# Latent weights summed by contiguous adds on two engines, and value products in fewer, larger batches

## The chip, the cores and the metric

The kernel runs on one core of one Trainium2 chip. The metric is device time in microseconds (us). Engines are named as in the profile: PE (TensorE's products), PEld (its weight loads), DVE (VectorE), ACT (ScalarE), POOL (GpSimd) and SP (SyncE, which issues all DMAs here). A name such as SPq means that engine's queue.

## The reference

One layer of a hybrid trunk over 1024 latent tokens (a grid of 16 rows by 64 columns) and 256 context tokens, width 1024, in float32: a gated feed-forward half step, two token mixers side by side, a merge, and a second half step. The two mixers matter here. Neighbourhood attention has 8 heads of width 64; each query attends to a window of 8 x 16 tokens and to all context tokens. Latent attention has 8 heads; each of the 1024 queries attends to all 1280 keys:

```python
def _attend(q, k, v):
    s = jnp.einsum('bqhd,bkhd->bhqk', q * q.shape[-1] ** -0.5, k).astype(jnp.float32)
    p = jax.nn.softmax(s, axis=-1).astype(v.dtype)
    return jnp.einsum('bhqk,bkhd->bqhd', p, v)
```

The kernel computes the softmax's denominator beside the value product, and divides at the end.

## The kernel before, in words

The program is written in Tile: a step-by-step plan fixes the order on some engines, and the framework orders the rest by priority and readiness and places all waits. PE's products are pinned to the order in which the program names them, and so are the DMAs on SP. The latent loop's operations on DVE, ACT and Pool that are called as `nc.vector`, `nc.scalar` and `nc.gpsimd` are not pinned.

**The latent stage** (about 1473 to 1790 us of the profile) works through 16 items, two per head, each with 512 queries. Keys lie on the partitions: an item has ten key blocks of 128, and so ten steps, kb = 0 to 9. A step does this:

- `scores(kb)`: three products into a PSUM bank ("bs", three banks), then on ACT the exponential into one of ten 128x512 parts (L1979). Five parts share one buffer X of 128x2560; there are four such buffers.
- one product for the maxima of a later item into a bank "bm" (three banks, shared with transposes), and DVE's reduction of it (L1938). An item has ten of them. The last one that item i+1 needs comes in step 4 of item i.
- `follow(i, kb)`: whatever is due at this step. In the kernel before: at step 0 the previous item's `total` (a strided sum of its parts 5 to 9 on DVE, L1993, and the add of Pool's sum of parts 0 to 4, L1994); at step 2 the previous item's second half of the value products, `weigh(1)`, and the products of the total with ones, which lay the denominator out for the division; at step 4 its `out` (reciprocal L2010 and product L2011 on DVE, then copies and subtractions on ACT and Pool); at steps 1 to 4 Pool's adds of the item's own parts (L1989); at step 5 the next item's `shift`, three short DVE operations over its maxima (L1957 to L1959); at step 6 its `row`, and then the first half of the own value products, `weigh(0)`.
- `row()` turns the shift into a row by a PE transpose (L160), copies it on DVE (L1966) and sends it by four small DMAs into row 96 of the query tile. The next item's first score product reads that row.

A value product multiplies a part (two halves of 256 queries) with 64 value columns, and the two halves go to the two halves of the PSUM bank's partitions ("bv", two banks). Each is seen as two entries in the profile, so that five parts show as x20.

**The neighbourhood stage** (about 1345 to 1470 us) works through 32 items, one per head and block of 16 query columns. A pair of items shares an X buffer and a bank "bv". An item transposes its weights in three parts (`local`, `context`, `edge`), copies them to SBUF tiles and remembers the value products as jobs. When the item's three parts are done and two more parts have followed, its `weigh` does the jobs, 20 entries of PE. Behind the odd item of a pair follows the pair's `out`. Scores of later items stand between the parts.

Durations named here for the stages are read off the timeline.

Of the kernel before, what the change touches and what calls it, by code (L numbers as in the profile page):

```python
# [12 lines left out]
ALU = mybir.AluOpType  # L13
AX = mybir.AxisListType

P = 128
# [22 lines left out]
def f32(ap):  # L39
    return ap.bitcast(F32)  # L40
# [3 lines left out]
def hybrid_block(ctx: ExitStack, tc: tile.TileContext, a: dict, out: bass.AP):  # L44
    nc = tc.nc
# [10 lines left out]
    def nm(s):  # L56
        count[0] += 1
        return f"{s}_{count[0]}"
# [17 lines left out]
    def T2(dt=F32, n=512):  # L76
        return pools["t"].tile([P, n], dt, tag="t", name=nm("t"))
# [13 lines left out]
    def PB(tag):  # L91
        return ps.tile([P, 512], F32, tag=tag, name=nm("b" + tag), bufs=PBUFS[tag])
# [22 lines left out]
    class Engine:  # L115


        def __init__(self, e):
            self.e = e
# [36 lines left out]
    def mmul(o, s, m, start, stop):  # L156
        return pin(nc.tensor.matmul(o, s, m, start=start, stop=stop, skip_group_check=open_group[0]))  # L157

    def turn_(o, x, i):
        return pin(nc.tensor.transpose(o, x, i))  # L160
# [96 lines left out]
    ones = strip[:, 1:2]  # L257
# [1017 lines left out]
    def emit_cq(i, ci, x, bank):  # L1275

        t, q = x, T2()
        if bank:
            t = T2()
            act.copy(t, x)  # L1280
        act.activation(q, t, AF.Square)
        if ci in sq:
            vec.tensor_tensor(sq[ci], sq[ci], q, op=ALU.add)
        else:
            sq[ci] = q
        store(cqx[i, :, ci * 512:(ci + 1) * 512], t)
# [22 lines left out]
    for p in range(3):  # L1309
        punits.append(Unit(h2, [cq_src(2 * p), cq_src(2 * p + 1)],  # L1310
                           lambda i, ci, x, bank, p=p: emit_cq(2 * p + i, ci, x, bank)))
# [451 lines left out]
    def weigh(pv, c, vts, pts, start, stop):  # L1763


        open_group[0] = True
        for e in range(2):
            n = pts[e].shape[-1]
            mmul(pv[64 * e:64 * e + 64, c:c + n], vts[e], pts[e], start, stop)
        open_group[0] = False  # L1770
# [3 lines left out]

    class NaPair:
        def __init__(self):
            self.x, self.pv = None, []

        def scores(self, n):
            if n < EARLY:  # L1780
# [26 lines left out]
    na_pairs = [NaPair() for _ in range(NH * 2)]  # L1807

    class NaItem:
# [38 lines left out]
        def weigh(self, last=True):  # L1848
            pv = na_pairs[self.n // 2].bank(self.n)
            for i, (vts, t) in enumerate(self.jobs):  # L1850
                weigh(pv, (self.n % 2) * P, vts, (t[:, 0:P], t[:, P:2 * P]), not self.begun, last and i == len(self.jobs) - 1)
                self.begun = True
            self.jobs = []

        def values(self):
            hd, j, h, pr = self.head, self.j, self.head.h, self.pr
            vt = lambda g: hd.v[:, j * 256 + g * 64:j * 256 + g * 64 + 64]
            vc = lambda g: f32(hd.kvc[:, 256 + g * 64:320 + g * 64])

            def turned(blocks, t, eng, tag="m"):  # L1860
                n = P * len(blocks)
                pb = PB(tag)
                for x, (s, kb) in enumerate(blocks):
                    turn_(pb[:, x * P:(x + 1) * P], pr[s][:, kb * P:(kb + 1) * P], ident)
                (nc.scalar.copy if eng else nc.vector.tensor_copy)(t[:, :n], pb[:, :n])

            def local():
                t = T2()
                turned(((0, 1), (1, 0), (0, 2), (1, 1)), t, 1, "m" if self.n else "v")
                self.jobs += [((vt(1 + e),) * 2, t[:, e * 256:(e + 1) * 256]) for e in range(2)]  # L1870

            def context():
                t = T2()
                turned(((0, 3), (1, 3), (0, 4), (1, 4)), t, 0, "s" if self.n == 1 else "m")
                self.jobs += [((vc(e),) * 2, t[:, e * 256:(e + 1) * 256]) for e in range(2)]

            def edge():
                t = T2()
                turned(((0, 0), (1, 2)), t, 1)
                self.jobs.append(((vt(0), vt(3)), t))  # L1880
                return [self.weigh] + ([lambda: na_pairs[self.n // 2].out(self.n, h, j)] if self.n % 2 else [])

            return [local, context, edge]

# [40 lines left out]
    class MlaItem:  # L1925
# [58 lines left out]
        def add(self, kb):  # L1984


            if kb == 1:
                self.acc = T2()
            nc.gpsimd.tensor_tensor(self.acc, self.part(0) if kb == 1 else self.acc, self.part(kb), op=ALU.add)  # L1989

        def total(self):
            self.l = T2()
            nc.vector.tensor_reduce(self.l, self.pt[1].rearrange("p (k q) -> p q k", k=5), axis=AX.X, op=ALU.add)  # L1993
            nc.vector.tensor_tensor(self.l, self.l, self.acc, op=ALU.add)  # L1994

        def weigh(self, half):
            if half == 0:
                self.pv = PB("v")
            for kb in range(5 * half, 5 * half + 5):
                v = self.hd.v[:, kb * 64:(kb + 1) * 64]  # L2000
                x = self.part(kb)
                weigh(self.pv, 0, (v, v), (x[:, 0:256], x[:, 256:512]), kb == 0, kb == 9)
            if half:
                v = ones.to_broadcast([P, 64])
                weigh(self.pv, 256, (v, v), (self.l[:, 0:256], self.l[:, 256:512]), True, True)

        def out(self):
            t, h, pv = T2(), self.hd.h, self.pv
# [142 lines left out]
    def follow(i, kb):  # L2151


        prev = mla[i - 1] if i else None
        item = mla[i] if i < len(mla) else None
        after = mla[i + 1] if i + 1 < len(mla) else None
        if kb == 0 and prev:
            prev.total()
        if kb == 0 and i % 2 == 0 and i // 2 + 1 < NH:
            mla_heads[i // 2 + 1].second()  # L2160
        if kb == 2 and prev:
            prev.weigh(1)
        if kb == 4 and prev:
            prev.out()
        if item and 1 <= kb < 6:
            item.add(kb) if kb < 5 else None
        if after and kb == 5:
            after.shift()
        if kb == 5 and i % 2 and i // 2 + 2 < NH:
            mla_heads[i // 2 + 2].first()  # L2170
        if after and kb == 6:
            after.row()
        if item and kb == 6:
            item.weigh(0)

    for i, item in enumerate(mla):
        for kb in range(10):
            item.scores(kb)
            next(tops, None)
            if i == 0:  # L2180
                finish_one()
                if pending and kb % 2 == 0:
                    ending += pending.pop(0)
            follow(i, kb)
            if i >= 14 and kb == 0:
                fm.load(i - 14)
            if i >= 14 and kb == 5:
                fm.split()
    for kb in range(5):
        follow(len(mla), kb)  # L2190
        for _ in range(3 if kb < 2 else 2):
            if fm.left:
                fm.step()
# [264 lines left out]
```

## Time and profile before

| what | value |
|---|---|
| runs | 2585.33, 2587.09, 2595.04 us; median 2587.09 |
| profiled execution | 2595.56 us, its span 2593.8 us |
| granted TensorE clock | 0.991 mean |
| busy | PE 97%, DVE 73%, ACT 43%, POOL 10% |
| chain that ended last | PE 87%, DVE 9%, ACT 2% |

The busy shares are means over stages with different limits, so they tell little of the latent stage alone. In a row of the timeline stand start, duration, engine, line, operation, the tile written and those read, shape and count, and in brackets how long the engine stood idle before it and who released it. Line L157 is the helper of all products and L123 that of pinned operations; the tiles tell them apart.

### The profile page before, as it was taken

Reading aid. Unit: us, or ns where it says so; the run is one execution under the profiler, and the core shown is the slowest. Engines: PE = TensorE matmul, PEld = TensorE weight load, DVE = VectorE, ACT = ScalarE, POOL = GpSimd, SP = SyncE. Lnnn points to the kernel's source line nnn. Section 1 sums busy time; section 2 is a strip of 40 time slices with the busy share of each in tenths; the row PEclk is TensorE's granted clock in tenths of the full one; section 3 lists DMA queues with packets and bytes.
Section 4 is the critical chain, followed back from the end, with each engine's and each line's share of the span. In section 5 each row is a group of like instructions: output and inputs, shape, how many; then the busy total and the mean of one; then the engine's idle time right before and its main releaser. Section 6 shows DMA issues by size and latency. Waiting matters only on the chain.

```text
span 2593.8 us, 36835 instructions
## 1 busy us (share of the span) xinstructions
PE 2521.7 (97%) x13176; PEld 2073.4 (80%) x13176; DVE 1893.2 (73%) x3146; ACT 1121.3 (43%) x2007; POOL 255.3 (10%) x368
## 2 busy tenths in 40 slices
PE   8999999999999999999999988889999999999998
PEld 6888888888998888888888755556888888888887
DVE  4789986797775578863557677676886888767777
ACT  5633223446654753433537533332167322333444
POOL 1000000001100000001003344332011000000003
PEclk9999999999999999999999999999999999999999
DMA  8555543943664666765867422214846444336824
GB/s 303 157 175 192 190 151 126 340 134 130 235 257 155 238 217 208 257 212 125 269 230 246 131 53 55 53 29 173 314 159 227 150 159 158 114 107 222 282 71 162
DMA packets 247671, 464.73 MB, mean 179 GB/s; under 512 B 61056, under 2 KB 77632, under 8 KB 247488
## 3 DMA queue, kind: packets, MB, share of 16 engines
q1 hardware_dynamic: 247488, 462.38, 53.3%
q8 instruction: 104, 1.70, 0.3%
q14 instruction: 79, 0.65, 0.1%
HBM read 341.59 MB, written 120.65 MB: 178 GB/s over the span
## 4 chain that ended last, share of the span: by engine, by line
PE 87%; DVE 9%; ACT 2%; issue 1%; DMA 1%; SPq 0%; POOL 0%; POOLq 0%; DVEq 0%; ACTq 0%
PE bs L157 37%; PE bm L157 27%; PE bv L157 20%; DVE t L1993 3%; DVE st L1938 2%; PE bm L160 2%; DVE t L2010 1%; PE bs L160 1%; ACT t L123 1%; DVE xv L123 1%; DVE xu L123 1%; ACT xu L123 0%; DVE t L1994 0%; DVE t L123 0%; PE bv L160 0%
## 5 line engine op out<-in xcount | busy, mean ns | idle before, releaser
L123 ACT CAST xu<-t 128x512 fp32r<-128x512 f32 (+1 forms) x270 | 160.9, 601 | 494.1 <-DVE t L123 352.4
L157 PE MATMUL bm<-xu,xu 128*128 128x512 f32 (+2 forms) x1572 | 366.5, 386 | 0.0
L157 PE MATMUL bs<-xv,xu 128*128 128x512 f32 x1488 | 357.3, 389 | 0.3 <-DVE t L123 0.3
L157 PE MATMUL bv<-xv,xu 128*128 128x512 f32 x1342 | 335.5, 389 | 0.0
L157 PEld LDWEIGHTS bm<-xu,xu 128*128 128x128 f32 x1572 | 288.1, 188 | 56.6 <-ACT t L123 0.2
L157 PEld LDWEIGHTS bs<-xv,xu 128*128 128x128 f32 x1488 | 279.2, 188 | 59.0 <-issue 1.1
L157 PEld LDWEIGHTS bv<-xv,xu 128*128 128x128 f32 x1342 | 251.8, 188 | 52.2
L157 PE MATMUL bs<-xv,xv 128*128 128x512 f32 x1086 | 265.8, 390 | 0.0
L123 DVE TENSOR_TENSOR xu<-xu,xu 128x512 fp32r<-128x512 f32 (+1 forms) x296 | 201.9, 687 | 74.3 <-ACT xu L123 74.0
L157 PEld LDWEIGHTS bs<-xv,xv 128*128 128x128 f32 x1086 | 203.0, 188 | 41.7
L157 PE MATMUL bs<-xu,xu 128*128 128x512 f32 (+1 forms) x972 | 226.2, 382 | 0.0
L123 POOL TENSOR_SCALAR st<-st 128x1 f32<-128x1 f32 (+1 forms) x66 | 34.7, 526 | 1884.3 <-ACT t L123 1866.0
L123 DVE TENSOR_TENSOR t<-t,t 128x512 f32<-128x512 f32 (+2 forms) x278 | 185.2, 673 | 45.0 <-ACT t L123 35.7
L157 PEld LDWEIGHTS bs<-xu,xu 128*128 128x128 f32 x972 | 177.4, 188 | 35.7 <-issue 1.4
L157 PE MATMUL bs<-w,w 96*128 96x512 f32 (+1 forms) x736 | 197.0, 384 | 1.9 <-DMA w<-kr 1.3
L123 DVE TENSOR_TENSOR xu<-t,xu 128x512 fp32r<-128x512 f32 (+1 forms) x270 | 179.3, 664 | 10.7 <-ACT xu L123 10.6
L1979 ACT ACTIVATE xp<-bs 128x512 f32<-128x512 f32 x160 | 95.5, 597 | 205.1 <-PE bs L157 204.5
L157 PE MATMUL bm<-xv,xv 128*128 128x512 f32 x690 | 182.8, 390 | 0.0
L123 ACT CAST xv<-t 128x512 fp32r<-128x512 f32 x170 | 105.7, 622 | 167.0 <-PE bv L157 69.2
L123 DVE TENSOR_TENSOR xv<-t,xv 128x512 fp32r<-128x512 f32 x170 | 117.0, 688 | 65.4 <-ACT xv L123 65.0
L123 ACT CAST xu<-xu 128x512 fp32r<-128x512 f32 x218 | 132.6, 618 | 67.4 <-DMA xu<-in_wo 54.3
L1938 DVE TENSOR_REDUCE st<-bm 128x1 f32<-128x512 f32 (+1 forms) x160 | 105.7, 679 | 74.3 <-PE bm L157 74.3
(242 smaller groups left out, 3935.9 us busy)
## 6 DMA issues: line engine op xcount, KB each, us to landing
d<-t SPq DMA_DIRECT2D x366, 256.0 KB, 2.6
t<-d SPq DMA_DIRECT2D x274, 256.0 KB, 3.7
xu<-in_f1w SPq DMA_DIRECT2D x59, 512.0 KB, 4.1
xu<-in_f2w SPq DMA_DIRECT2D x58, 512.0 KB, 3.9
t<-in_wada SPq DMA_DIRECT2D x112, 256.0 KB, 5.0
xv<-in_f1w SPq DMA_DIRECT2D x44, 512.0 KB, 6.8
xu<-in_winT SPq DMA_DIRECT2D x38, 512.0 KB, 4.8
xu<-in_f1w SPq DMA_DIRECT2D x50, 256.0 KB, 5.4
```

What stands on the lines that cost most here:

```text
L123: return lambda *x, **y: pin(f(*x, **y))
L157: return pin(nc.tensor.matmul(o, s, m, start=start, stop=stop, skip_group_check=open_group[0]))
L160: return pin(nc.tensor.transpose(o, x, i))
L1938: nc.vector.tensor_reduce(d[:, c:c + pb.shape[-2]], pb, axis=AX.X, op=ALU.max)
L1979: nc.scalar.activation(self.part(kb), pb, AF.Exp)
L1993: nc.vector.tensor_reduce(self.l, self.pt[1].rearrange("p (k q) -> p q k", k=5), axis=AX.X, op=ALU.add)
L2010: nc.vector.reciprocal(rb, pv[:, 256:512])
```

## The change

In the latent stage the denominator's sum is spread: Pool adds parts 0 to 6 as they come (six adds instead of four), DVE adds parts 7, 8 and 9 by contiguous adds and then Pool's sum (three adds in place of the strided sum and one add). Each own part is added one step later. The value products of an item are no longer split in two halves at step 6 of the item and step 2 of the next; all ten parts and the products with ones come in one batch at step 3 of the next item. In the neighbourhood stage both items of a pair do their value products together, when the odd item's turn comes.

```diff
     class NaPair:
         def __init__(self):
-            self.x, self.pv = None, []
+            self.x, self.pv, self.items = None, [], []
+
+        def weigh(self):
+            for x in self.items:
+                x.weigh()
...
-                return [self.weigh] + ([lambda: na_pairs[self.n // 2].out(self.n, h, j)] if self.n % 2 else [])
+                pair = na_pairs[self.n // 2]
+                pair.items.append(self)
+                return [pair.weigh, lambda: pair.out(self.n, h, j)] if self.n % 2 else []
...
         def add(self, kb):
+            p = self.part(kb)
             if kb == 1:
                 self.acc = T2()
-            nc.gpsimd.tensor_tensor(self.acc, self.part(0) if kb == 1 else self.acc, self.part(kb), op=ALU.add)
+                nc.gpsimd.tensor_tensor(self.acc, self.part(0), p, op=ALU.add)
+            elif kb < 7:
+                nc.gpsimd.tensor_tensor(self.acc, self.acc, p, op=ALU.add)
+            elif kb == 8:
+                self.l = T2()
+                nc.vector.tensor_tensor(self.l, self.part(7), p, op=ALU.add)
+            elif kb > 8:
+                nc.vector.tensor_tensor(self.l, self.l, p, op=ALU.add)
 
         def total(self):
-            self.l = T2()
-            nc.vector.tensor_reduce(self.l, self.pt[1].rearrange("p (k q) -> p q k", k=5), axis=AX.X, op=ALU.add)
             nc.vector.tensor_tensor(self.l, self.l, self.acc, op=ALU.add)
 
-        def weigh(self, half):
-            if half == 0:
-                self.pv = PB("v")
-            for kb in range(5 * half, 5 * half + 5):
+        def weigh(self):
+            self.pv = PB("v")
+            for kb in range(10):
                 v = self.hd.v[:, kb * 64:(kb + 1) * 64]
                 x = self.part(kb)
                 weigh(self.pv, 0, (v, v), (x[:, 0:256], x[:, 256:512]), kb == 0, kb == 9)
-            if half:
-                v = ones.to_broadcast([P, 64])
-                weigh(self.pv, 256, (v, v), (self.l[:, 0:256], self.l[:, 256:512]), True, True)
+            v = ones.to_broadcast([P, 64])
+            weigh(self.pv, 256, (v, v), (self.l[:, 0:256], self.l[:, 256:512]), True, True)
...
         if kb == 0 and prev:
+            prev.add(9)
             prev.total()
...
-        if kb == 2 and prev:
-            prev.weigh(1)
+        if kb == 3 and prev:
+            prev.weigh()
         if kb == 4 and prev:
             prev.out()
-        if item and 1 <= kb < 6:
-            item.add(kb) if kb < 5 else None
+        if item and kb > 1:
+            item.add(kb - 1)
...
-        if item and kb == 6:
-            item.weigh(0)
```

## The prediction

> **What bounds the kernel now.** I read the page first (span, busy shares, the chain that ended last), then stretches of the two attention stages, then the waits and the timeline of one latent item.
>
> ```profile
> span 2593.8 us, 36835 instructions
> ...
> PE 2521.7 (97%) x13176; PEld 2073.4 (80%) x13176; DVE 1893.2 (73%) x3146; ACT 1121.3 (43%) x2007; POOL 255.3 (10%) x368
> ...
> PE 87%; DVE 9%; ACT 2%; issue 1%; DMA 1%; SPq 0%; POOL 0%; POOLq 0%; DVEq 0%; ACTq 0%
> PE bs L157 37%; PE bm L157 27%; PE bv L157 20%; DVE t L1993 3%; DVE st L1938 2%; PE bm L160 2%; DVE t L2010 1%; PE bs L160 1%; ACT t L123 1%; DVE xv L123 1%; DVE xu L123 1%; ACT xu L123 0%; DVE t L1994 0%; DVE t L123 0%; PE bv L160 0%
> ```
>
> TensorE is the bound nearly everywhere. The exception is DVE's 9% of the chain, and its largest piece is L1993, the strided sum that goes. The next rows tell the stages apart (PE, PEld, DVE, ACT, POOL busy, granted clock, DMA share, GB/s): the first lies in the neighbourhood stage, the second in the latent one.
>
> ```profile
> 1385.00:1405.00 20.00, 20.00 (x206) 17.69 (x204) 13.79 (x59) 14.97 (x37) 5.58 (x11) 1.00 0.76 257
> ```
> ```profile
> 1690.00:1755.00 65.00, 53.55 (x280) 35.12 (x277) 47.75 (x60) 19.35 (x34) 24.01 (x27) 0.92 0.07 16
> ```
>
> The neighbourhood stage has PE busy for all its 20 us: only PE's own time can be saved there. In the latent stage PE stands still for 11.45 us of 65, and the clock is at 0.92. The waits of that stage name the two stops, and three rows of operations its rate and the sum's cost (the copy at L1966 runs once per item, so its first and last start give the period):
>
> ```profile
> PE bm L160 <- DVE st L1959: 24.9, 15, 2.0
> PE bv L157 <- DVE t L1994: 23.0, 15, 1.8
> ```
> ```profile
> L1966 DVE COPY kr<-bm x15: 269/279/279, 1483.9 to 1759.0; 4x128 f32<-4x128 f32 x15
> L1993 DVE TENSOR_REDUCE t<-xp x16: 4680/4718/4729, 1489.8 to 1780.2; 128x512 f32<-128x2560 f32 x16
> ```
> ```profile
> L1994 DVE TENSOR_TENSOR t<-t,t x16: 677/681/693, 1495.0 to 1785.0; 128x512 f32<-128x512 f32 x16
> ```
>
> The period is (1759.0 - 1483.9) / 14 = 19.65 us. Once per item PE waits for the total of the weights (L1994, behind L1993's 4.72 us), once for the shift of the next item (L1959), which PE has to transpose. One item in the timeline:
>
> ```profile
> 1566.37 0.86 PE L157 MATMUL bs<-w,w 97*128 97x512 f32 x3
> ...
> 1569.26 2.38 PE L157 MATMUL bv<-xp,w 128*64 128x256 f32 x20
> ...
> 1573.14 0.65 PE L157 MATMUL bv<-t,strip 128*64 128x256 f32 x4 [1.51 <-DVE t L1994]
> ...
> 1573.73 0.97 PE L157 MATMUL bs<-w,w 97*128 97x512 f32 x3
> 1574.20 1.75 DVE L2010 RECIPROCAL t<-bv 128x256 f32<-128x256 f32 x1
> ...
> 1575.87 1.22 DVE L1938 TENSOR_REDUCE st<-bm 128x1 f32<-128x512 f32 x2
> ...
> 1576.64 0.86 PE L157 MATMUL bs<-w,w 97*128 97x512 f32 x3
> ...
> 1577.00 0.42 DVE L2011 TENSOR_TENSOR t<-bv,t 128x256 f32<-128x256 f32 x1
> ...
> 1577.93 0.16 DVE L1957 TENSOR_REDUCE st<-st 128x4 f32<-128x8 f32 x1
> ...
> 1578.60 0.16 DVE L1958 TENSOR_TENSOR st<-st,st 128x4 f32<-128x4 f32 x1
> 1578.79 0.36 DVE L1959 TENSOR_SCALAR st<-st 128x4 f32<-128x4 f32 x1
> ...
> 1579.30 0.27 PE L160 MATMUL bm<-ident,st 128*4 128x128 f32 x1 [1.56 <-DVE st L1959]
> ...
> 1579.50 4.05 PE L157 MATMUL bv<-xp,w 128*64 128x256 f32 x20
> ```
>
> The reader is to see a loop through two engines: ones product (1573.14), reciprocal, maxima, shift, transpose. After the stop at 1579.30 the same 20 value products take 4.05 us that took 2.38 at 1569.26: the clock is halved, 1.67 us lost. The stage's 0.92 means 0.08 x 65 = 5.2 us of full speed lost, 1.6 per item.
>
> **The change, part by part.** I call the ten rounds of an item steps 0 to 9.
>
> *The sum.* L1993's 4.72 us and its add become three contiguous DVE adds. L1994 is that kind of add, 0.68 us, so 2.0 us instead of 5.4; Pool gets six adds instead of four. One of the DVE adds falls behind step 9 and two behind step 0 of the next item, where the value batch now follows at step 3: PE has some 8 us of its own work (four steps and 40 products, below) before the ones product needs the total. The stop of 1.51 us goes, at a cost of nothing, and the cover is those 8 us; Pool's sum may come 2 us late before three PSUM banks of maxima are full and PE feels it.
>
> *One value batch per item.* The slope of a batch comes from these rows and the four ones products above:
>
> ```profile
> 1540.87 2.38 PE L157 MATMUL bv<-xp,w 128*64 128x256 f32 x20
> ...
> 1543.18 0.96 PE L157 MATMUL bs<-w,w 97*128 97x512 f32 x3
> ```
>
> 20 products to the next kind: 2.31 us; 4 products: 0.59 (1573.14 to 1573.73); so 0.1075 each and 0.16 for leaving the batch. 44 together take 4.89. Three steps take 2.89 us (1566.37 to 1569.26), four 3.85. From the start of step 0 to the start of step 4 the new item needs 3.85 + 4.89 = 8.74 us.
>
> *The turn of the shift.* It stays at step 6, three steps behind the ones product instead of four: PE reaches it 2.91 us after step 4 starts. DVE's way is longer. The reciprocal started 0.47 us after the following step, behind leftover maxima; now these are done during the batch, so 0.1. Then 1.67 for it, 0.57 for one maximum (two took 1.13), 0.93 for product and maximum (1577.00 to 1577.93), 1.37 from L1957 to the turn: 4.64 us. Unlike L1994's, this stop is not removed; the head of the queue on DVE is still the reciprocal, with the maxima and PE's turn behind it. What Pool does to it:
>
> ```profile
> 1481.37 1.29 POOL L1989 TENSOR_TENSOR t<-t,xp 128x512 f32<-128x512 f32 x1 [1.08 <-ACT xp L1979]
> ```
> ```profile
> 1481.86 0.82 DVE L1958 TENSOR_TENSOR st<-st,st 128x4 f32<-128x4 f32 x1
> ```
>
> L1958, 0.16 us alone, lasts until Pool's add ends. Adds 4 to 6 now lie in this stretch, at 1.29 us each. Bounds for the turn: 2.91 (DVE in time) and 4.64 + 2 x 1.29 = 7.2 (L1958 and L1959 each blocked by a whole add). I take 4.95, 0.3 above the undisturbed way, since a head's short copies and subtractions on Pool are as likely to meet the shift as an add. [...]
>
> *The row behind the turn.* Formerly 20 value products stood between the turn and steps 7 to 9; now only the steps do, and step 0 of the next item reads the transposed row, which goes by DVE copy and four DMAs on SP's queue. The trace shows this distance uncovered once, ahead of the first item:
>
> ```profile
> 1468.50 0.27 PE L160 MATMUL bm<-ident,st 128*4 128x128 f32 x1 [0.70 <-DVE st L1959]
> ...
> 1469.16 2.47 SPq L135 DMA_DIRECT2D w<-kr  x4
> ...
> 1472.93 0.94 PE L157 MATMUL bs<-w,w 97*128 97x512 f32 x3 [1.35 <-DMA w<-kr]
> ```
>
> 4.43 us from turn to scores. PE has 0.2 + 2.9 = 3.1 us of work for it: a new stop of 1.33 us per item, which takes the place of the one removed. Bounds 3.1 and 4.43 + 1.67 (half clock behind it) = 6.1; I take 4.43, the row itself. The head loads on SP stand behind the row's DMAs, not ahead of them, so SP adds nothing.
>
> *The clock.* A stop of 2 us at the turn will still halve the clock in perhaps six items of ten, but the slow steps 7 to 9 are then waiting for the row anyway: 1.67 - 1.33 = 0.34 is left, 0.2 on average. [...]
>
> *Sum of the latent stage.* 8.74 + 4.95 + 4.43 + 0.2 = 18.32 us against 19.65: 1.33 x 14 = 18.6 us. The last item has no turn and loses only its stop, 1.8 us by this row:
>
> ```profile
> 1769.72 0.65 PE L157 MATMUL bv<-t,strip 128*64 128x256 f32 x4 [1.79 <-DVE t L1994]
> ```
>
> Together 20.4 us.
>
> *Pairs in the neighbourhood stage.* 32 batches become 16, each exit worth 0.16: 2.6 us. In exchange the passage from an odd to an even item has no products:
>
> ```profile
> 1397.81 0.84 PE L157 MATMUL bs<-w,w 128*128 128x256 f32 x4
> ...
> 1398.58 1.31 PE L157 MATMUL bv<-t,w 128*64 128x128 f32 x20
> ...
> 1399.65 0.42 DVE L1773 TENSOR_SCALAR_CACHE_REDUCE xp<-bs 128x256 f32<-128x256 f32 x1
> ...
> 1399.82 0.88 PE L160 MATMUL bm<-ident,xp 128*128 128x128 f32 x6
> ```
>
> DVE has the scores out of PSUM at 1400.07. Without the batch PE would want the next scores at 1398.58 + 0.88 = 1399.46 at the latest; if it had to wait for that evacuation, 0.6 x 15 = 9 us would be lost. The banks are given out as they come free, and the first one needed is freed an evacuation earlier, so I take a gain of 2 us, with ends at a gain of 2.6 and a loss of 6.4.
>
> Total: 22.4 us. The profiled execution took 2595.56 us, its span and 1.8 us around it, and lies 8.5 above the median of 2587.09; from it the sum gives 2573, from the median **2565 us**.
>
> **The rivals.**
> *The turn is free too.* If the shift's operations go ahead of the reciprocal on DVE, the turn is at 2.91 and the period 8.74 + 2.91 + 4.43 = 16.1: 3.55 x 14 + 1.8 + 2 = 53.5 us, 2534. For it: four short operations that need only step 4's maximum. Against: at 1574.20 the reciprocal goes first, though two maxima are due in the program before it.
> *Pool eats half.* L1959 waits for one whole add: turn at 5.9, period 19.3, gain 0.35 x 14 + 1.8 + 2 = 9 us, 2578. For it: 1481.86. Against: at 1578.60 and 1578.79 the shift ran undisturbed.
> *Slower.* Both small operations meet a fresh add in every item: turn at 7.2. PE then stands for 4.3 us at the turn and the half clock is certain: period 8.74 + 7.2 + 4.43 + 0.34 = 20.7, 1.06 x 14 - 3.8 = 11 us slower, 2598, and up to 2618 if the row's stop brings another 1.67 with it. It decides from a turn 6.3 us behind step 4 (19.65 - 8.74 - 4.43 - 0.2). Against: six adds of 1.29 fill only 7.7 us of an 18 us item.
> *The sum is not shortened where it counts.* The total waits for Pool's sixth add; it must be over 2 us late to show, and then gives the second rival's time.
>
> **How the numbers follow.** The forecast has 0.55, the free turn 0.13, Pool's half 0.20, slower 0.12. 2565 is the likeliest. The range goes from 2540 to 2594: it leaves out most of the free turn (0.10) and most of the slower case (0.10). 0.5% is 13 us, about what a measurement can tell from no change. Faster by more: 0.50 of the forecast, 0.13, and 0.02 of Pool's half, 0.65; within: 0.05 + 0.18 + 0.04, 0.27; slower: 0.08.
>
> **What would show it.** Right: no L1993; 48 DVE adds of some 0.68 us; PE waits for the total gone; PE at the turn still waits for L1959, about 2 us, 15 times; a new wait of PE's scores for the row's DMA, about 1.3 us in most items; L1966's period 18.3; the neighbourhood stage full as before. Wrong: no wait for the row or at the turn (then faster), L1958 and L1959 lengthened to a microsecond by Pool (slower), gaps of PE in the neighbourhood stage.

## The result, and the profile after

The changed kernel takes 2583.39 us (median of 18 runs, 2579.33 to 2586.79), the kernel before on the same chip 2590.08 us (18 runs, 2585.18 to 2595.44). The ratio is 0.9975, with a 95% interval of 0.9967 to 0.9982: 6.7 us faster, where 22.4 were forecast. The new profiled execution took 2584.02 us, 0.6 above its median; the profiled execution before lay 5.5 above the median of these 18 runs.

The page after, in its span, busy and chain rows:

```profile
span 2582.2 us, 36926 instructions
...
PE 2513.7 (97%) x13176; PEld 2080.6 (81%) x13176; DVE 1853.8 (72%) x3162; ACT 1124.1 (44%) x2007; POOL 301.0 (12%) x400
...
PE 90%; DVE 4%; ACT 2%; DMA 2%; issue 1%; SPq 1%; POOL 0%; DVEq 0%; POOLq 0%; ACTq 0%
PE bs L157 38%; PE bm L157 28%; PE bv L157 21%; PE bm L160 2%; DVE t L2020 1%; DVE st L1944 1%; PE bs L160 1%; ACT t L123 1%; SPq L135 1%; DMA w<-kr 1%; DVE xu L123 0%; ACT xu L123 0%; DVE st L1964 0%; ACT xv L123 0%; PE bv L160 0%
```

DVE's 9% of the chain are now 4%, and L1993 is gone from it. SPq has grown from 0% to 1%, and the row's DMA (`w<-kr`), not among the rows before, has 1%. The same two stretches as before, one in each stage:

```profile
1385.00:1405.00 20.00, 19.79 (x209) 17.76 (x206) 13.95 (x61) 16.08 (x39) 6.92 (x14) 1.00 0.59 197
1690.00:1755.00 65.00, 55.13 (x273) 39.42 (x275) 37.11 (x57) 22.14 (x39) 35.97 (x35) 0.85 0.09 28
```

In the neighbourhood stage PE is no longer quite full (19.79 of 20 us). In the latent stage PE is busy for longer and its clock is lower, 0.85 against 0.92. PE's waits there from 1475 to 1790 us (total, times, longest), and three groups of DVE's operations (shortest/median/longest ns, first and last start):

```profile
PE bm L160 <- DVE st L1965: 27.6, 15, 3.0
PE bs L157 <- DMA w<-kr: 11.8, 8, 3.0
```
```profile
L1972 DVE COPY kr<-bm x15: 269/278/279, 1483.2 to 1744.8; 4x128 f32<-4x128 f32 x15
L1964 DVE TENSOR_TENSOR st<-st,st x15: 152/811/1143, 1481.2 to 1742.6; 128x4 f32<-128x4 f32 x15
L1965 DVE TENSOR_SCALAR st<-st x15: 153/170/1045, 1482.5 to 1743.0; 128x4 f32<-128x4 f32 x15
```

The wait for the total (23.0 us before) is gone. The wait at the turn has grown from 24.9 to 27.6 us, and a wait for the row has come. The copy runs once per item: the period is (1744.8 - 1483.2) / 14 = 18.69 us, where it was 19.65 and 18.32 was forecast. L1964, the shift's two-input maximum, takes 0.81 us in the median, five times its shortest.

Two items in the timeline, with the rows that set their length:

```profile
1541.09 0.95 PE L157 MATMUL bs<-w,w 97*128 97x512 f32 x3 [1.24 <-DMA w<-kr]
...
1549.87 0.96 PE L157 MATMUL bs<-w,w 97*128 97x512 f32 x3
...
1551.61 2.63 POOL L1998 TENSOR_TENSOR t<-t,xp 128x512 f32<-128x512 f32 x2 [3.94 <-ACT xp L1985]
...
1553.13 1.13 DVE L1964 TENSOR_TENSOR st<-st,st 128x4 f32<-128x4 f32 x1
...
1555.08 0.27 PE L160 MATMUL bm<-ident,st 128*4 128x128 f32 x1 [2.15 <-DVE st L1965]
...
1559.40 0.94 PE L157 MATMUL bs<-w,w 97*128 97x512 f32 x3 [1.26 <-DMA w<-kr]
...
1568.18 0.96 PE L157 MATMUL bs<-w,w 97*128 97x512 f32 x3
...
1571.27 1.20 POOL L123 MEMSET w<- 1x1024 f32 x2
1571.44 0.15 DVE L1964 TENSOR_TENSOR st<-st,st 128x4 f32<-128x4 f32 x1
...
1572.63 0.27 PE L160 MATMUL bm<-ident,st 128*4 128x128 f32 x1 [1.39 <-DVE st L1965]
...
1576.93 0.94 PE L157 MATMUL bs<-w,w 97*128 97x512 f32 x3 [1.23 <-DMA w<-kr]
```

The four marks of the forecast are all there: step 0 (1541.09), step 4 (1549.87, 8.78 us later), the turn (1555.08, 5.21 later), the next step 0 (1559.40, 4.32 later). In the second item Pool runs only a memset beside L1964, which takes 0.15 us, and the turn comes 4.45 us behind step 4. So of two items at full clock one takes 18.31 us with Pool's add in the way and the next 17.53 without.

A third item shows two more things:

```profile
1590.41 1.26 POOL L1998 TENSOR_TENSOR t<-t,xp 128x512 f32<-128x512 f32 x1
1590.65 1.04 DVE L1965 TENSOR_SCALAR st<-st 128x4 f32<-128x4 f32 x1
...
1591.84 0.37 PE L160 MATMUL bm<-ident,st 128*4 128x128 f32 x1 [3.04 <-DVE st L1965]
...
1597.14 1.48 PE L157 MATMUL bs<-w,w 97*128 97x512 f32 x3
```

L1965, which has one input, lasts until Pool's add ends, too. And the three steps behind the 3.04 us stop run at half clock (0.50 granted from 1591.84 to 1597.14): the next step 0 comes 5.30 us behind the turn instead of 4.3, with no wait for the row.

### The profile page after: what moved, and what is told of

It reads as the page before. It is cut to its first block, busy times and chain, and to the rows that moved or that the text cites. A ratio compares the mean times of both kernels' runs of the same rounds, so it can differ in the third digit from the quotient of the medians.

```text
span 2582.2 us, 36926 instructions
## 1 busy us (share of the span) xinstructions
PE 2513.7 (97%) x13176; PEld 2080.6 (81%) x13176; DVE 1853.8 (72%) x3162; ACT 1124.1 (44%) x2007; POOL 301.0 (12%) x400
## 4 chain that ended last, share of the span: by engine, by line
PE 90%; DVE 4%; ACT 2%; DMA 2%; issue 1%; SPq 1%; POOL 0%; DVEq 0%; POOLq 0%; ACTq 0%
PE bs L157 38%; PE bm L157 28%; PE bv L157 21%; PE bm L160 2%; DVE t L2020 1%; DVE st L1944 1%; PE bs L160 1%; ACT t L123 1%; SPq L135 1%; DMA w<-kr 1%; DVE xu L123 0%; ACT xu L123 0%; DVE st L1964 0%; ACT xv L123 0%; PE bv L160 0%
## 5 line engine op out<-in xcount | busy, mean ns | idle before, releaser
L157 PE MATMUL bs<-w,w 96*128 96x512 f32 (+1 forms) x736 | 210.7, 405 | 16.3 <-DMA w<-kr 13.6
L157 PEld LDWEIGHTS bs<-w,w 96*128 96x128 f32 (+1 forms) x736 | 132.4, 205 | 45.1 <-issue 16.3
```

## The experiments

The theory (A): the contiguous sum does take a stop away, but the one batch at step 3 gives most of that back, by a shift that now waits on DVE behind the division and Pool's adds, and by a row whose DMA no products cover. Its rivals: the half clock eats the gain (B); the adds themselves cost what they save (C).

All results, with the period worked out as above and the stretches of half clock from 1470 us to the end of the latent stage, 3.41 us each, counted in the clock's records:

| kernel | median us | ratio to before, interval | period us | half-clock stretches |
|---|---|---|---|---|
| before | 2590.08 | 1 | 19.65 | 12 |
| changed | 2583.39 | 0.9975, 0.9967 to 0.9982 | 18.69 | 14 |
| na_only | 2593.09 | 1.0007, 0.9998 to 1.0015 | 19.63 | 12 |
| mla_only | 2583.47 | 0.9960, 0.9946 to 0.9973 | 18.82 | 14 |
| batch_only | 2581.41 | 0.9962, 0.9949 to 0.9974 | 18.79 | 3 |
| sum_only | 2556.61 | 0.9872, 0.9857 to 0.9887 | 17.03 | 1 |
| late_out | 2573.33 | 0.9933, 0.9916 to 0.9950 | 17.82 | 7 |
| short_shift | 2564.16 | 0.9897, 0.9880 to 0.9914 | 17.12 | 6 |
| late_batch | 2579.81 | 0.9958, 0.9943 to 0.9973 | 18.40 | 14 |
| late_short | 2545.81 | 0.9821, 0.9802 to 0.9839 | 15.64 | 5 |
| sum_out | 2574.80 | 0.9936, 0.9919 to 0.9953 | 18.63 | 12 |
| sum_short | 2530.11 | 0.9762, 0.9744 to 0.9780 | 15.42 | 1 |
| before_warm | 2580.87 | 0.9960, 0.9945 to 0.9975 | 18.68 | 3 |
| after_warm | 2581.25 | 0.9959, 0.9947 to 0.9971 | 18.36 | 8 |

The medians of before were 2589.8 to 2592.7 us in the sets of runs of these kernels.

**The baseline.** The kernel before once more (before_look).

> The kernel before, unchanged, for a second profile. Theory B (the baseline: the execution that the prediction summed against was a slow one of its kind, with many half-clock stretches in the latent stage): 2588 to 2591 us, some 9 or 10 half-clock stretches in the latent stage instead of 12, and a latent period of 19.3 us or less, so that 4 to 5 us of the missing gain were never there. Theories A and C (the missing gain lies in the changed kernel): a period of 19.6 us again and the same number of stretches.

One execution, 2593.7 us: a period of 19.54 us and 11 stretches instead of 19.65 and 12. This execution too was above the median, so it doesn't decide; the 18 runs do, by which the profiled one was 5.5 us slow.

**The parts of the change.** na_only is before with the pairs' batch alone, mla_only the changed kernel without it:

```diff
...
-                pair = na_pairs[self.n // 2]
-                pair.items.append(self)
-                return [pair.weigh, lambda: pair.out(self.n, h, j)] if self.n % 2 else []
+                return [self.weigh] + ([lambda: na_pairs[self.n // 2].out(self.n, h, j)] if self.n % 2 else [])
```

> Kernel before with the one batch per neighbourhood pair alone; the latent stage is as before. The prediction's step: 2 us faster (between 2.6 faster and 6.4 slower). Theory A (what the pair saves in exits comes back as waits of the batch and of its loads, as the pair period in the trace after, 7.51 against 7.57 us over 14 pairs, says): 0 to 2 us faster, 2588 to 2590. Rival: the pair's batch costs what the latent stage gains, 10 us or more slower, 2600.

> The changed kernel with the neighbourhood pairs as before, so that the whole difference to it is the pair's one batch. The prediction's step (the pairs gain 2 us): 2585.4 us, 2 us slower than the changed kernel. Theory A (what the pair saves in exits comes back as waits, as the kernel with the pairs alone said, 0.07% slower than before): 2580 to 2584 us, no slower than the changed kernel.

The pairs gain nothing: 2593.09 us against 2589.8, an interval that holds no change and no gain over 0.02%; and without them the changed kernel takes 2583.47 us (0.9960 of before), no more than with them (0.9975).

sum_only keeps the two half batches and takes the new adds; batch_only keeps the strided sum and takes the batch at step 3. The edit of sum_only against the changed kernel (the pairs are as before, too):

```diff
...
-        if kb == 3 and prev:
-            prev.weigh()
+        if kb == 2 and prev:
+            prev.weigh(1)
...
+        if item and kb == 6:
+            item.weigh(0)
```

> Kernel before with the contiguous adds on Pool and DVE alone; both value batches stay in two halves, at step 2 and behind the row at step 6. Theory A (the sum does take the stop for the total away, and the one batch at step 3 is what gives most of it back, because it pushes the shift behind the reciprocal and leaves the row's DMA without products that cover it): 1.3 to 1.7 us less per period than before, 18 to 25 us faster, 2565 to 2572, and faster than the changed kernel by 10 us or more. Theory C (the adds themselves are what gives the gain back: Pool's six adds end late and hold DVE's two-input adds): no faster than the changed kernel, 2583 or above.

> Kernel before with the latent batch whole at step 3 alone; the strided sum over five blocks stays on DVE and Pool adds four blocks, and the neighbourhood pairs are as before. Theory A: the batch alone moves the total out of the way (its products come 4 us later) but brings the stops at the turn and at the row, so 2578 to 2592 us, within 0.4% of the changed kernel. Theory C: the batch alone is the whole gain and the adds cost some: 2575 or less. Rival: without the adds the strided sum of 4.7 us still holds the maxima behind it, and the two stops of the batch come on top: 2600 or more.

The sum alone makes the kernel 33 us faster, 8 more than expected and 27 us faster than the whole change. The batch alone gives 2581.4 us, no worse than the whole change: with the batch at step 3 it hardly matters how the sum is made. The waits of batch_only show why:

```profile
PE bs L157 <- DMA w<-kr: 19.5, 15, 1.9
PE bm L160 <- DVE st L1959: 18.5, 15, 1.4
PE bm L157 <- DVE st L1938: 12.7, 12, 1.1
```

No wait for the total: the late batch hides even the strided sum. But the row, the turn and the maxima behind that sum stop PE instead. Those of sum_only:

```profile
PE bm L160 <- DVE st L1959: 26.5, 15, 2.2
PE bs L157 <- DMA w<-kr: 0.5, 1, 0.5
```

One stop is left, at the turn, and the row costs nothing, since 20 products lie behind it. That 33 us is more than the 23.0 us of the stop removed leads to the clock. Before's stretches fall from 12 to 1. Each cost 1.67 us there (the prediction's 4.05 against 2.38), so 11 x 1.67 + 23.0 = 41.4 us; the two profiled spans differ by 2593.8 - 2551.1 = 42.7, more than the medians do, since before's profiled execution lay above its median and sum_only's was the shortest of its four. C is out.

**The clock.** Useless products ahead of each transpose shorten the pause there without a change to what follows: six in after_warm, five in before_warm, where PE's wait at the turn falls from 24.9 to 6.4 us.

```diff
             pt = PB("m")
+            for _ in range(6):
+                mmul(pt, self.hd.kh[:QK, 0:P], self.hd.kh[:QK, 0:512], True, True)
             turn_(pt[:4, :P], self.n_, ident)
```

> The kernel before with five such products ahead of each transpose, 1.1 us of a stop of 1.6 to 2.0 us; the stop for the total stays. Theory D (the strided sum's price is 1.5 us of stop and the half clock on top, because in the kernel before no row's wait absorbs the slow products, and so the contiguous adds alone gained 33 us and not 20): stretches fall from 11 or 12 to 4 or fewer, 12 to 18 us faster than before, 2572 to 2578 us. Rival (the 33 us are another thing, such as the maxima held behind the strided sum): 2585 us or more.

> The changed kernel with six more products of 512 columns, of no use, into the transpose's bank ahead of each transpose, 1.3 us of a stop that lasts 1.3 to 3.2 us there. They end before the shift does, so they delay nothing, and they keep PE's pauses under 2 us. Theory A (the half clock costs the changed kernel little, 0.5 us per item, since the slow steps would wait for the row anyway): half-clock stretches fall from 14 to 4 or fewer and the time by 5 to 10 us only, 2573 to 2579 us. Theory B (the half clock is the main part of the missing gain): 2568 us or less. If the stretches stay 10 or more, pauses of this kind are not what sets the clock.

In before, the stretches fall from 12 to 3, and the profiled span by 15.0 us, which is 9 x 1.67; in the medians 12 us. So the half clock is a price of its own there, on top of the stops. In the changed kernel the stretches only fall from 14 to 8 and the time by 2 us, less than expected; the row's wait takes the place of the slow products:

```profile
PE bs L157 <- DMA w<-kr: 16.2, 12, 2.6
PE bm L160 <- DVE st L1965: 8.7, 7, 1.6
```

That is 16.2 us for the row where the changed kernel had 11.8, and 8.7 at the turn where it had 27.6. B foresaw 2568 us or less. So the half clock is not the main part of the missing gain; as eight stretches are left, the run doesn't say that it costs nothing, and its share is worked out further down.

**The turn.** short_shift is the changed kernel with the maxima in one tile of twelve columns and the shift in one operation:

```diff
...
-            n_, u = ST(4), ST(4)
-            nc.vector.tensor_reduce(u, self.m.rearrange("p (t e) -> p t e", t=4), axis=AX.X, op=ALU.max)
-            nc.vector.tensor_tensor(u, u, self.mc, op=ALU.max)
-            nc.vector.tensor_scalar(n_, u, -1.0, None, op0=ALU.mult)
+            n_ = ST(4)
+            nc.vector.tensor_reduce(n_, self.m.rearrange("p (t e) -> p t e", e=3), axis=AX.X, op=ALU.max, negate=True)
```

> The changed kernel with the shift as one negated maximum over twelve columns instead of a maximum, a two-input maximum and a product by -1; nothing moves. Theory A3 (Pool's adds, of over a microsecond each, hold the shift's small two-input operation, and so make the turn late in half of the items): from the start of step 4 to the turn 3.9 to 4.2 us in all items instead of 4.24 to 6.11, 2562 to 2572 us. Rival (a late turn costs nothing because the three steps behind it wait for the clock anyway): 2579 to 2584 us.

19 us faster than the changed kernel. Its shift and its waits:

```profile
L1964 DVE TENSOR_REDUCE st<-t x15: 152/154/156, 1485.7 to 1724.9; 128x4 f32<-128x12 f32 x15
```
```profile
PE bs L157 <- DMA w<-kr: 24.9, 16, 3.4
PE bm L160 <- DVE st L1964: 6.8, 14, 0.5
```

Pool adds as often as in the changed kernel, but the reduction never lasts over 0.156 us, where the two-input operation took up to 1.143. The stop at the turn falls from 27.6 to 6.8 us. The turn now comes 3.56 us behind step 4; in the changed kernel it took 4.24 to 4.46 where no add of Pool was in the way, and up to 6.11 where one was. So some 0.8 us go with the two operations that are gone, and the rest was Pool's.

In the changed kernel's trace L1964 is long only where an add of Pool (L1998) was running when it began: that was so nine times of 15, it took 0.38 to 1.14 us, and it ended within 0.03 us of that add's end each time. Beside a memset it took 0.15 to 0.16. That one input is no protection by itself L1965 shows, a TENSOR_SCALAR that ended with Pool's add in the same way four times, with 1.04 to 1.05 us. The reduction L1963, which has one input too, began inside such an add 15 times and took 0.16 each time. What tells the two apart, no run shows.

What is left is the row, 24.9 us in 16 items. Turn and row together fall by 7.7 us only (39.4 to 31.7); the rest of the 19 goes along with fewer stretches of half clock, 6 instead of 14.

late_out moves the division to step 6, behind the row, in the changed kernel; sum_out does the same in sum_only:

```diff
-        if kb == 4 and prev:
+        if kb == 4 and prev and not after:
             prev.out()
...
         if after and kb == 6:
             after.row()
+            if prev:
+                prev.out()
```

> The changed kernel with the division (reciprocal and product) moved from step 4 to step 6, behind the next item's shift and row; the batch stays at step 3, so the row's DMA still has only three steps to hide it. Theory A1 (the division ahead of the shift on DVE holds PE's transpose, and this stop is also what halves the clock): from the start of step 4 to the turn 3.0 to 3.5 us instead of 5.1, fewer half-clock stretches than 8, a period of 16.4 to 17.0 against 18.69, and 2552 to 2564 us. Theory A2 (the uncovered row is what counts): the earlier turn only lengthens the wait for the row, which stays 4.4 us behind the turn; a period of 18.0 or more and 2574 us or more.

> The kernel with the contiguous adds and the two half batches (2556.6 us), with the division moved from step 4 to step 6, behind the shift and the row and ahead of the first half batch of the next item. Theory A1: its one stop, 1.7 us per item at the turn, goes: a period of 15.2 to 15.7 against 17.03, 2533 to 2541 us. Rival (the stop at the turn is the shift's own time on DVE, not the division's): a period of 16.5 or more, 2550 us or more.

late_out gains 10 us, half of the least that was expected, and sum_out loses 18 where 15 to 24 were expected as a gain. DVE's order in sum_out shows that the edit did not do what it says:

```profile
1567.54 1.76 DVE L2016 RECIPROCAL t<-bv 128x256 f32<-128x256 f32 x1 [0.75 <-PE bv L157]
...
1572.06 0.15 DVE L1958 TENSOR_TENSOR st<-st,st 128x4 f32<-128x4 f32 x1
1572.13 0.42 DVE L2017 TENSOR_TENSOR t<-bv,t 128x256 f32<-128x256 f32 x1
1572.47 0.37 DVE L1959 TENSOR_SCALAR st<-st 128x4 f32<-128x4 f32 x1
```

DVE isn't pinned, and the framework still takes the reciprocal as soon as its input is there, ahead of the shift; only its product moved, into the middle of the shift. The stop at the turn grew (33.9 us against 26.5), and the stretches came back, 12 against 1. In late_out, too, the reciprocal still goes ahead of the shift; PE waits for the turn for 18.9 us instead of 27.6, but for the row for 18.9 instead of 11.8. So neither kernel tells what a division really behind the shift would give; that stays open.

**The row.** late_batch puts the whole batch behind the row, late_short has the short shift too:

```diff
-        if kb == 3 and prev:
-            prev.weigh()
-        if kb == 4 and prev:
+        if kb == (8 if after else 4) and prev:
             prev.out()
...
         if after and kb == 6:
             after.row()
+        if kb == (6 if after else 3) and prev:
+            prev.weigh()
```

> The changed kernel with the whole batch at step 6, behind the row, and the division at step 8; for the last item both stay where they were. Neither stop of the batch is left: the shift has no division ahead of it, and the row's 4.4 us pass under 44 products. Theory A (these two stops and the half clock that they bring are all that the batch costs): ten steps at 0.96 us, 4.89 us of products and the transpose make a period of 14.9 to 15.5, 2532 to 2542 us. Rival (DVE and Pool bind an item before PE does): a period of 16.5 or more, 2556 us or more.

> The kernel with the whole batch at step 6 behind the row (2579.8 us), with the short shift. Its turn waits on DVE, which gets nothing to do during the 5 to 6 us of products and then has division, three adds and ten maxima to do in ten short steps. Theory A4 (Pool's add in front of the shift and the half clock behind it are the smaller part, DVE's backlog the larger): the turn still stops PE by over 0.5 us in most items, 2550 to 2565 us, worse than the two half batches with the same shift. Rival (the stop was Pool's doing alone): period 15.5 or less, 2542 us or less.

late_batch came out 38 us above the upper end of its expectation. The row is covered (1.2 us of waits for it), but the turn stops PE for 31.3 us, and the maxima for 5.0. DVE's queue in one item (rows without a bracket follow the one before without a pause):

```profile
1576.98 1.76 DVE L2020 RECIPROCAL t<-bv 128x256 f32<-128x256 f32 x1 [6.07 <-PE bv L157]
...
1583.12 2.36 DVE L2006 TENSOR_TENSOR t<-t,t 128x512 f32<-128x512 f32 x1
1585.40 2.47 DVE L1944 TENSOR_REDUCE st<-bm 128x1 f32<-128x512 f32 x4
...
1588.46 0.86 DVE L1964 TENSOR_TENSOR st<-st,st 128x4 f32<-128x4 f32 x1
1589.35 0.17 DVE L1965 TENSOR_SCALAR st<-st 128x4 f32<-128x4 f32 x1
```

DVE stands still for 6.07 us during the batch, and is then busy without a break from 1576.98 to 1589.5, with two operations that take longer than elsewhere: L2006 takes 0.69 us in the changed kernel, and L1964 0.15 at its shortest. With the short shift the same order takes 2545.8 us, between its two expectations: the stop at the turn falls from 31.3 to 7.1 us and the stretches from 14 to 5, so the long shift and the half clock behind it were the larger part there, and not, as the theory had it, DVE's backlog. Against short_shift, which differs in the place of batch and division, it is 18.4 us faster. The wait for the row falls from 24.9 to 1.7 us, and 5.0 us of waits for the maxima come in.

**Both mended.** sum_short is sum_only with the short shift.

> The kernel with the contiguous adds and the two half batches (2556.6 us), with the shift as one negated maximum over twelve columns. Theory A3 (what is left of its stop, 27 us in all at the turn, is mostly the shift's small operations and Pool's add in front of them): the stop falls to 10 us in all or less, a period of 15.8 to 16.2 against 17.03, 2536 to 2545 us. Rival (the turn waits for the division and the maxima, however short the shift): 2550 us or more.

2530.11 us, 0.9762 of before (0.9744 to 0.9780): 53 us faster than the changed kernel, and better than expected. All that PE waits for in the latent stage:

```profile
PE bv L157 <- DVE t L1999: 2.4, 3, 0.8
PE bm L160 <- DVE st L1958: 2.1, 13, 0.2
PE bs L157 <- DMA w<-kr: 0.3, 1, 0.3
```

15.7 us lie between this kernel and late_short with its one batch. The likely reason, which no run isolates, is that with two half batches DVE can catch up twice per item, and the one behind the turn covers the row as well.

## Why the prediction was wrong, by its own steps

The mechanism was the forecast's: the stop for the total went, the turn kept its stop, the row got a new one. The net of these was put at 22.4 us and came to 6.7. What failed are terms of the sum: the half clock, put at 0.2 us per item, cost 0.56; the last item was put at a gain and lost; the pairs gained nothing; and the base was an execution 5.5 us above its median. The missing 15.7 lie in these terms, by the two profiled executions and the runs:

- *Sum of the latent stage, 18.6 us forecast, (19.65 - 18.69) x 14 = 13.5 measured: 5.1 missing.* By the marks shown above, read in the 13 items behind the first, step 0 to step 4 took 8.97 us in the mean (8.74 forecast), step 4 to the turn 5.09 (4.95), the turn to the next scores 4.68 (4.63 with the half clock's 0.2). Where no half clock fell, the first took 8.78 and the last 4.31. So the row itself cost 0.12 less than its 4.43, and the half clock 0.19 + 0.37 = 0.56 where 0.2 was put: 0.36 x 14 = 5.0 us, the size of what is missing here. The forecast let the wait for the row take up most of one slow slice of 3.41 us. But ten of the 14 slices come in pairs: four times all three steps behind the turn are slow and take 5.29 us, longer than the row, and what is left of a pair, or once a whole slice, falls on steps 0 to 3, where no wait takes it up.
- *The turn: right in the mean, by luck.* It is made up otherwise: 4.24 to 4.46 us where Pool's adds stay away (4.64 forecast), 5.2 or 6.1 where they don't, in 7 of the 13 items. The forecast gave Pool 0.3 us on the average; it costs L1964 alone 0.66 in the median item, and in four items L1965 some 0.9 more. In those four items an add held each of the two operations, as the prediction's upper bound had it, but that bound of 7.2 us was never reached (6.11 at most).
- *The last item, 1.8 us forecast as a gain.* The last item has no turn, but it reads a row, and the forecast left that out:

```profile
1743.18 1.65 DVE L123 TENSOR_TENSOR w<-t,w 128x512 fp32r<-128x512 f32 x1
...
1743.29 0.27 PE L160 MATMUL bm<-ident,st 128*4 128x128 f32 x1 [0.79 <-DVE st L1965]
...
1744.76 0.27 DVE L1972 COPY kr<-bm 4x128 f32<-4x128 f32 x1
...
1748.70 5.41 PE L157 MATMUL bs<-w,w 97*128 97x512 f32 x12 [3.03 <-DMA w<-kr]
```

  No maxima are left to fill the steps here, and the row's copy waits behind an operation of the next stage on DVE: it starts 1.47 us behind the transpose, where 0.37 is usual. So the row stops PE for 3.03 us, and the half clock follows for two slices. From the last copy (L1966, now L1972) to the last reciprocal 27.4 us became 30.4: 3.0 lost instead of 1.8 gained, 4.8 missing. The first period, from the first turn to the second, 15.0 us before and 16.1 after, loses another 1.1; it was not forecast at all.
- *Pairs, 2 us forecast.* Nothing, by two runs. The exits saved come back as pauses of PE: from 1345 to 1466 us it is busy for 117.91 us instead of 119.27, and stands still for 3.09 instead of 1.73.
- *The base.* The gain was worked out on an execution that was 5.5 us slower than the median run, and then taken off a median. Of the 11.5 us between the two profiled executions, 4.9 are this difference (5.5 - 0.6) and not the change's. The prediction had both figures, 2573 from the profiled execution and 2565 from the median, and took the one to which the sum did not belong.

Together 5.1 + 4.8 + 1.1 + 2.0 + 4.9 = 17.9; the 2.2 over are the profiled execution's lead of 1.7 us at the first turn (1466.76 against 1468.50), 0.3 behind the last reciprocal, and rounding. As kernels with the pairs' batch and without it reach the first turn 1465.9 to 1469.9 us after the start, that lead is not the pairs'.

What held: the new stop at the row. From the turn to the next scores it was 4.31 us where no half clock fell, 4.43 in the forecast, and PE waited for the row for 1.2 to 1.3 us in seven items; in most of the others the half clock filled the time. That covering the row brought 18.4 us (late_short against short_shift), near the forecast's 1.33 x 14 = 18.6, is partly chance, since that run moves the division and adds a wait as well. Of the rivals, Pool eating half came nearest with 2578 us, and its mechanism was at work in about half of the items; but its turn of 5.9 us was not the mean, so this too is near by luck.

What the prediction did not weigh at all: its 22.4 us were the net of a large gain and a large loss, and only the net was given chances. The sum alone was worth 33 us and not the 23 of its stop, because with that stop the stretches of half clock fell as well, from 12 to 1; the batch lost 27 of them.

## What to carry to other kernels

Where a change joins two moves, sum each alone before the net: here one was worth 33 us and the other took 27 back, and the version that keeps only the first, with a one-operation shift, is 53 us faster than both together. A block of products is also a cover, for a DMA behind it (PE waited for the row for 0.5 us in sum_only and for 11.8 in the changed kernel) and for an engine that has to catch up (the 23.0 us of waits for DVE's total are gone behind the one batch); before two small blocks are joined, list what each of them hid. And a short operation on DVE lasted here, in some items, until the end of an add that Pool had begun before it: one with two inputs (1.14 us instead of 0.15) and one with a single input (1.04 instead of 0.15). On a path to TensorE, fold such operations into one that the trace shows undisturbed; here that was a reduction (0.156 us at most in 15 items).

## What the runs showed of the hardware

In the profiles of the two kernels the half clock comes in slices of a fixed grid. By the clock's records, all its stretches in one profile begin whole multiples of 3.413 us apart, to within 0.03 us, 14 of them before and 10 after (some of two slices); two neighbours in the kernel before, by busy times and granted clock (0.51 and 0.50):

```profile
1580.00:1583.40 3.40, 3.40 (x18) 1.63 (x14) 0.00 (x0) 0.00 (x0) 1.71 (x3) 0.51 0.03 5
1583.40:1600.50 17.10, 13.55 (x75) 9.49 (x75) 14.68 (x18) 6.26 (x11) 7.23 (x8) 1.00 0.18 43
1600.50:1603.90 3.40, 3.40 (x18) 1.58 (x14) 0.00 (x0) 0.00 (x0) 0.00 (x0) 0.50 0.02 1
```

In the kernel before, by PE's busy times, PE stood still for 1.35 to 2.04 us of the slice ahead of each of the 12 stretches of the latent stage. All seven slices with more than 1.6 us were followed by one; of those with 1.35 to 1.6 us five were and thirteen were not, so these times show no sharp limit.

The place of a stop on the grid seems to count, too. sum_only stops PE at the turn for 26.5 us in 15 items, 1.57 to 2.24 us in each of the six turns from 1498.02 to 1584.30, and has one stretch only, in which 20 value products at 1549.35 take 3.62 us instead of 2.38. Its period of 17.03 us is nearly five slices (17.07), so its stops stay near one place on the grid, and by the grid laid out from that stretch these six lie across a border of two slices (1582.06 to 1584.30 with the border at 1582.62): no slice holds over 1.68 us of them. In the kernel before, 11 of the last 14 stops at the turn lie within one slice, and from 1638 to 1740 us its stretches follow each other at 20.5 us, six slices (20.48). That the place on the grid is the cause is argued from these numbers; no run moved it. It fits that the times of the kernels with stops spread by 3.5 to 10.3 us from run to run, and those of sum_short, which has hardly any, by 1.5 (2528.81 to 2530.27, 4 runs).
